# Mixer layer on one core: the dt stage placed in the u projection, conv token work emitted later, Fourier steps started later

## The chip, the cores and the metric

The kernel runs on one core of a Trainium2 chip. The metric is the device time in microseconds (us). A core has a matrix engine (TensorE, PE in the profile), a vector engine (DVE), a scalar engine (ACT), GpSimd (POOL) and SyncE (SP), which in this kernel issues all the DMA transfers. Each engine runs its own queue of instructions in order, and waits at an instruction whose inputs, or whose output buffer, are not ready.

## The reference

One layer with two parallel groups of channels: a Fourier group and a bidirectional chunked scan (SSD). The context, 256 tokens, only feeds the scan's starting states. Cut to what matters:

```python
u, zf, zs, xbc, dt_raw = jnp.split(h @ w_in, PROJ_SPLITS, axis=-1)   # h: normed, modulated tokens
four = fourier_mixer(u, zf, w_fourier, b_fourier)    # Re(fft2(u)) @ w_f + b_f, times silu(zf)
xbc = depthwise_conv_grid(xbc, conv_w, conv_b, rows, cols)           # 3x3 taps, then silu
# ssd_mixer, x/B/C from xbc, two directions:
dt = jax.nn.softplus(dt_raw + dt_bias)
A = -jnp.exp(a_log)
a_cum = jnp.cumsum(dt * A, axis=-1)                  # inside each chunk of 128 tokens
y_diag = einsum(cb, exp(segsum(a)), x * dt)
states = einsum(B, exp(a_cum[..., -1:] - a_cum), x * dt)
y_off = einsum(C, previous_states, exp(a_cum))
y = y_f + flip(y_b) + d_skip * x
out = rmsnorm(y * silu(zs)) * norm_w
x = x + gate * (concat([four, out]) @ w_out)         # then a final rmsnorm
```

There are 2048 latent tokens of width 1024, so 16 latent chunks and 2 context chunks of 128 tokens, and 24 heads in each of two directions (48 columns of dt).

## The kernel before

Data are fp32; a product with fp32 accuracy is made of three products of split operands (high part `h`, low part `l`), so a projection of one 128-wide weight tile onto 512 tokens is 8 x 3 matmuls, L170 to L172. The split of a weight tile (L72) has its high part on ACT and its low part (`wl<-raw,wh`) on POOL. All the work is emitted by one Python program; a scheduler with a model of time then sets the order of the instructions on each engine, and emission order is the priority among what it finds ready. The order on an engine is fixed when the program is built. PE writes to PSUM buffers by kind: five of kind `mm` (called pj or po in the rows), two of kind `tr` (ptr, L152), one of kind `cx`. Evacuation tiles `ev` (L179) and the weight tiles `wh`, `wl` have two buffers each, and these two buffers are used in turn.

The stages, in the order of time:

1. Norm, modulation, the raw dt projection (`dt_block`, which leaves dtT_d in DRAM), and the first two tiles of zf (L183 evacuates them).
2. The u projection, L373 to L393: 16 rounds `n2`. Each has 24 matmuls (L380 to L382), a split of the result, and a DFT group of three matmuls (L388 to L390) through a ptr buffer. At round 2 the context's norm is emitted.
3. The conv stage, L397 to L508: 20 tiles of 128 channels in the order CONV_ORDER, four groups of one C tile, one B tile and three x tiles. Each tile projects four blocks of 512 tokens into a padded image; `finish(half)` (L464) makes the nine taps (one on ACT, L467, eight on DVE, L470) into `acc` and the silu on ACT (L473). Then come the token parts: transposes on PE (L415, `to_tokens`) with an ACT copy to `tk` and a store to xtok_d; for B tiles also a split into `sh` and `sl` (ACT, then POOL) with stores to bhl_d, and the C·B products (L445). For C tiles the split and the stores to chl_d are made from acc. `sh` and `sl` hold eight chunks in one buffer each.
4. The dt stage, L522 to L610: all of dt for nine chunks at a time (NH = 9), two halves one after another, in pools of its own. Per half: dtT is loaded, a matmul a chunk with the matrix `i2` sums the high and low rows (L547; the trace has two records of each, 36 in all), about 15 steps on DVE and ACT make softplus, dt·A (`da`, L569), then the cumulative sums on PE (L572 with `triu` and `tril`, L575 with `ones`), exponentials, and 9 or 7 transposes each of `cum` and `lq` (L602), whose results go as `th` (ACT, L68) and `tl` (DVE, L606), one buffer each, to DRAM (cum_d, q_d), at most four chunks at a time. `sml` (state weights and total decay), `ecb` and `dsc` stay in SBUF for the scan; the whole is also stored to sm_d for the main stage.
5. The scan stage, L664 to L760: 16 context units and then 64 steps of the backward direction. A unit loads x and B, weighs x on POOL (`xw`, L686), splits it (`xh` on ACT, `xl` on DVE), and makes three matmuls of 384 columns (L716 to L718); POOL and DVE update the state (L725, L726). From the first latent chunk on, `scan_off` adds the output products (L698 to L700). The remaining zf and zs projections (`zs_ops`, L618) are emitted between the steps by `interleave` (L649) to fill PE.
6. The Fourier stage, L789 to L950: tables `f_table` (L835), the second DFT step, and the mixing products `f_mm`, interleaved with the last blocks of zs by the same function: `interleave(main, side, lead, speed)` emits the side steps only once `lead` microseconds of its modelled main work are out, and then at the rate `speed`.
7. The main stage: units that join the two directions and the output projection (L1008 to L1143).

Of the kernel before, what the change touches and what calls it, by code (L numbers as in the profile page):

```python
# [18 lines left out]
P = 128  # L19
# [7 lines left out]
H = 24  # L27
# [22 lines left out]
def mixer_layer(ctx: ExitStack, tc: tile.TileContext, A: dict, out: bass.AP, taps=None):  # L50
# [299 lines left out]
    with ExitStack() as pu:  # L350
# [46 lines left out]
    with ExitStack() as pc_:  # L397
# [28 lines left out]
        def hl_tiles():  # L426
            return [cp.tile([P, 8, P], F32R, name=nm, tag=nm, bufs=1) for nm in ("sh", "sl")]
# [27 lines left out]
        def conv_tile(n, ci):  # L455
# [8 lines left out]
            def finish(half):  # L464
# [10 lines left out]
                if kind == "x":  # L475
                    x_tokens(sof, j, c0, 8)
                elif kind == "B":
                    b_tokens(sof, j, c0, 8)
                    cb_products(sof, cso[half], j, c0)
                else:  # L480
                    cso[half] = sof
                    parts = hl_tiles()
                    split(*parts, sof.rearrange("p (c w) -> p c w", w=P), nc.gpsimd)
                    hl_store(chl_d, parts, c0, 8, j)
# [37 lines left out]
    pre1 = preload(LNEXP)  # L522
    with ExitStack() as pd, tc.issue_after(pre1):
        sm = pool("smd", stack=pd)
        tp = pool("tpd", stack=pd)
        triu = const_tile("triu", where=sm)
        tril = const_tile("tril", where=sm)
        ones = const_tile("ones", where=sm)
        alog = const_tile("alog", where=sm)
        dtb = const_tile("dtb", where=sm)  # L530
        i2 = const_tile("i2", where=sm)
        dsk = const_tile("dskip", where=sm)
        nega = sm.tile([P, W2], F32, name="nega")
        nc.scalar.activation(nega, alog, AF.Exp)
        nc.vector.tensor_scalar(out=nega, in0=nega, scalar1=-1.0, scalar2=None, op0=ALU.mult)
        NH = NALL // 2
        for hf_ in range(2):
            sl = slice(NH * hf_, NH * hf_ + NH)

            def small(tag):  # L540
                return tp.tile([P, NH, W2], F32, name="t_" + tag, tag=tag)

            dtT = tp.tile([2 * W2, NH * P], F32, name="dtT", tag="dtT", bufs=1)
            load(dtT, dtT_d[:, NH * P * hf_:NH * P * (hf_ + 1)])
            pt = tr_psum([P, NH, W2])
            for q in range(NH):
                mm(pt[:, q, :], dtT[:, q * P:(q + 1) * P], i2, start=True, stop=True)  # L547
            v, e, u, s1_, same, da, cum = (small(t) for t in ("v", "e", "u", "s1", "same", "da", "cum"))
            smx = tp.tile([P, NH, 2, W2], F32, name="smx", tag="smx", bufs=1)
            wdec, etot = (sml[:, sl, i] for i in range(2))  # L550
            ecum, dtt = (smx[:, :, i] for i in range(2))

            def bc(t):
                return t[:].unsqueeze(1).broadcast_to([P, NH, W2])

            nc.vector.tensor_tensor(out=v, in0=pt, in1=bc(dtb), op=ALU.add)
            nc.vector.scalar_tensor_tensor(out=e, in0=v, scalar=-1.0, in1=v, op0=ALU.mult, op1=ALU.max)
            nc.scalar.activation(e, e, AF.Exp, scale=-1.0)
            nc.vector.tensor_scalar(out=u, in0=e, scalar1=1.0, scalar2=None, op0=ALU.add)
            nc.scalar.activation(s1_, u, AF.Ln)  # L560
            nc.vector.tensor_scalar(out=u, in0=u, scalar1=-1.0, scalar2=None, op0=ALU.add)
            nc.vector.tensor_scalar(out=same, in0=u, scalar1=0.0, scalar2=None, op0=ALU.is_equal)
            nc.vector.tensor_tensor(out=u, in0=u, in1=same, op=ALU.add)
            nc.vector.tensor_tensor(out=s1_, in0=s1_, in1=same, op=ALU.add)
            nc.vector.reciprocal(out=u, in_=u)
            nc.vector.tensor_tensor(out=s1_, in0=s1_, in1=u, op=ALU.mult)
            nc.vector.tensor_tensor(out=s1_, in0=s1_, in1=e, op=ALU.mult)
            nc.vector.scalar_tensor_tensor(out=dtt, in0=v, scalar=0.0, in1=s1_, op0=ALU.max, op1=ALU.add)
            nc.vector.tensor_tensor(out=da, in0=dtt, in1=bc(nega), op=ALU.mult)  # L569
            for d, tri in enumerate((triu, tril)):  # L570
                pt = tr_psum([P, NH, H])
                mm(pt, tri, da[:, :, d * H:(d + 1) * H], start=True, stop=True)  # L572
                nc.vector.tensor_copy(out=cum[:, :, d * H:(d + 1) * H], in_=pt)
            pt = tr_psum([P, NH, W2])
            mm(pt, ones, da, start=True, stop=True)  # L575
            nc.scalar.activation(etot, pt, AF.Exp)
            nc.vector.tensor_tensor(out=wdec, in0=pt, in1=cum, op=ALU.subtract)
            nc.scalar.activation(wdec, wdec, AF.Exp)
            nc.vector.tensor_tensor(out=wdec, in0=wdec, in1=dtt, op=ALU.mult)
            nc.scalar.activation(ecum, cum, AF.Exp)  # L580
            lq = small("lq")
            nc.vector.tensor_scalar(out=lq, in0=dtt, scalar1=1e-37, scalar2=None, op0=ALU.max)
            nc.scalar.activation(lq, lq, AF.Ln)
            nc.vector.tensor_tensor(out=lq, in0=lq, in1=cum, op=ALU.subtract)
            c1 = min(NCH, NH * (hf_ + 1))
            nl, cl = c1 - NH * hf_, slice(NH * hf_, c1)
            nc.gpsimd.tensor_copy(out=ecb[:, cl], in_=ecum[:, :nl, H:])
            dv = dsc[:, cl]
            nc.vector.tensor_tensor(out=dv, in0=dtt[:, :nl, H:].rearrange("p c (g h) -> p c g h", g=G),
                                    in1=cbd[:, cl].unsqueeze(3).broadcast_to([P, nl, G, HG]), op=ALU.mult)  # L590
            dv = dv.rearrange("p c g h -> p c (g h)")
            nc.vector.tensor_tensor(out=dv, in0=dv, in1=dsk[:].unsqueeze(1).broadcast_to([P, nl, H]), op=ALU.add)
            store(sm_d[sl, :, 0:2].rearrange("c p i w -> p c i w"), sml[:, sl])
            store(sm_d[sl, :, 2:4].rearrange("c p i w -> p c i w"), smx)
            for src, dst in ((cum, cum_d), (lq, q_d)):
                c0 = NH * hf_
                while c0 < min(NH * (hf_ + 1), NCH):
                    nq = min(4, min(NH * (hf_ + 1), NCH) - c0)
                    n = nq * P
                    pt = tr_psum([W2, 512])  # L600
                    for q in range(nq):
                        nc.tensor.transpose(pt[:, q * P:(q + 1) * P], src[:, c0 + q - NH * hf_, :], ident)  # L602
                    th = tp.tile([W2, 512], F32R, name="th", tag="th")
                    tl = tp.tile([W2, 512], F32R, name="tl", tag="tl")
                    copy(th[:, :n], pt[:, :n])
                    nc.vector.tensor_tensor(out=tl[:, :n], in0=pt[:, :n], in1=th[:, :n].bitcast(F32), op=ALU.subtract)  # L606
                    cs = slice(c0 * P, c0 * P + n)
                    store(dst[0, :, cs].bitcast(F32), th[:, :n].bitcast(F32))
                    store(dst[1, :, cs].bitcast(F32), tl[:, :n].bitcast(F32))
                    c0 += nq  # L610
# [692 lines left out]
```

## Time and profile before

| | before |
|---|---|
| runs, median (lowest to highest) | 2002.3 us (1998.61 to 2002.57), 3 runs |
| the profiled execution, its own time | 1995.1 us |
| its span | 1993.2 us |
| stage 1 | 0 to 118 us, PE busy 98.69 |
| stage 2, u projection | 118 to 231 us, PE busy 113.00 of 113 |
| stage 3, conv | 231 to 806 us, PE busy 547.89 of 575 |
| stage 4, dt, to the first scan unit's weighing | 806 to 889 us, PE busy 51.19 of 83, mean clock 0.78 |
| stage 5, scan | 889 to 1187 us, PE busy 283.66 of 298, mean clock 0.94 |
| stage 6, Fourier | 1187 to 1340 us, PE busy 141.76 of 153 |
| stage 7, main units | 1340 to 1993.2 us, PE busy 599.58 of 653.2 |

All the rows come from one profiled execution; its times count from the start of its span. An engine is called busy while an instruction runs on it. A row of the timeline gives start, duration, engine, line, operation and tiles, and in brackets how long the engine stood idle before and what released it. The clock is the share of full TensorE speed that the chip granted. Matmuls overlap in the pipeline, so the distance between two starts, not the duration in a row, is the pace.

### The profile page before, as it was taken

How to read it: one execution, taken by the hardware profiler on the slowest of the kernel's cores; microseconds unless marked ns; L12 is line 12 of the kernel's file. 1: busy time of each engine (PE TensorE's matmuls, PEld its weight loads, DVE VectorE, ACT ScalarE, POOL GpSimd, SP SyncE). 2: the span in 40 equal slices, each digit the busy share in tenths (PEclk: the TensorE clock that was granted, in tenths of full speed). 3: DMA queues.
4: the chain of work that ended last, by engine and by line, in shares of the span. 5: the costliest groups of instructions: out<-in, count | busy, mean ns of one | idle time of the engine just before them, and what ended most of it. 6: DMA issues, size and time to landing. Idle time of an engine off the chain costs nothing.

```text
span 1993.2 us, 27660 instructions
## 1 busy us (share of the span) xinstructions
PE 1835.8 (92%) x9136; PEld 1507.1 (76%) x9136; DVE 1382.5 (69%) x1820; ACT 868.2 (44%) x1932; POOL 918.8 (46%) x760
## 2 busy tenths in 40 slices
PE   6999999999999999938999989988899999999997
PEld 2799987877878878726788877866687777778775
DVE  3742399898998998447667651247877787787874
ACT  3531143434443434325666653325544344444433
POOL 1321133131140241108777762247867676877742
PEclk8999999999999999957999999998899999999999
DMA  7332133232232332436777765466544444454441
GB/s 273 131 94 76 34 96 93 70 99 71 76 98 72 88 101 58 139 102 198 219 227 229 222 204 188 143 202 196 177 139 125 132 148 123 134 157 132 135 141 46
DMA packets 267679, 268.47 MB, mean 135 GB/s; under 512 B 27057, under 2 KB 235537, under 8 KB 267026
## 3 DMA queue, kind: packets, MB, share of 16 engines
q1 hardware_dynamic: 267538, 266.72, 44.2%
q8 instruction: 73, 1.20, 0.3%
q14 instruction: 68, 0.56, 0.1%
HBM read 180.10 MB, written 86.54 MB: 134 GB/s over the span
## 4 chain that ended last, share of the span: by engine, by line
PE 37%; DVE 7%; DMA 6%; POOL 3%; ACT 2%; issue 2%; SPq 1%; DVEq 0%; ACTq 0%; POOLq 0%
PE po L1143 5%; PE po L1142 5%; PE po L1141 5%; PE pj L170 4%; PE pj L172 4%; PE pj L171 4%; PE py L1082 2%; PE parg L1008 1%; DMA wo<-in_wout 1%; PE py L1085 1%; DMA xg<-xtok_d 1%; PE ptr L849 1%; SPq L63 1%; DVE gt L1107 1%; PE pn L1098 1%
## 5 line engine op out<-in xcount | busy, mean ns | idle before, releaser
L470 DVE SCALAR_TENSOR_TENSOR acc<-img,c_convw,acc 128x1024 f32<-128x1024 f32 x320 | 485.6, 1524 | 49.2 <-ACT acc L467 39.6
L172 PE MATMUL pj<-hh,wl 128*128 128x512 f32 x1152 | 455.4, 395 | 0.0
L171 PE MATMUL pj<-hl,wh 128*128 128x512 f32 x1152 | 454.4, 394 | 0.0
L170 PE MATMUL pj<-hh,wh 128*128 128x512 f32 x1152 | 453.5, 398 | 0.0
L72 POOL TENSOR_TENSOR wl<-raw,wh 128x1024 fp32r<-128x1024 f32 x48 | 122.9, 2561 | 402.8 <-ACT wh L68 402.8
L172 PEld LDWEIGHTS pj<-hh,wl 128*128 128x128 f32 x1152 | 218.5, 190 | 45.9 <-issue 0.5
L170 PEld LDWEIGHTS pj<-hh,wh 128*128 128x128 f32 x1152 | 219.4, 190 | 42.0 <-issue 1.8
L171 PEld LDWEIGHTS pj<-hl,wh 128*128 128x128 f32 x1152 | 218.6, 190 | 41.1 <-issue 2.1
L1141 PE MATMUL po<-hl,mh 128*128 128x512 f32 x384 | 156.2, 407 | 3.8 <-ACT mh L68 3.1
L1142 PE MATMUL po<-hh,mh 128*128 128x512 f32 x384 | 152.5, 397 | 3.9 <-DVE hh L786 3.9
L1143 PE MATMUL po<-hl,ml 128*128 128x512 f32 x384 | 146.7, 400 | 3.6 <-POOL ml L72 3.6
L703 ACT ACTIVATE xd<-xt,dsc 128x64 f32<-128x64 f32 x384 | 101.3, 336 | 75.9 <-POOL yb L706 69.8
L473 ACT ACTIVATE acc<-acc,c_convb 128x1024 f32<-128x1024 f32 x40 | 46.1, 1152 | 160.4 <-DVE acc L470 160.4
L1012 ACT ACTIVATE w<-parg 128x384 f32<-128x384 f32 x128 | 62.3, 487 | 110.0 <-DVE parg L1010 109.6
L1008 PE MATMUL parg<-rt,lt 128*128 128x384 f32 x256 | 89.6, 374 | 13.2 <-DVE parg L1010 7.0
L1013 DVE TENSOR_TENSOR w<-w,cb 128x768 f32<-128x768 f32 x64 | 85.9, 1342 | 13.1 <-ACT w L1012 12.3
L68 ACT ACTIVATE xh<-xw 128x384 fp32r<-128x384 f32 x136 | 70.2, 517 | 56.7 <-POOL xw L686 25.1
L72 POOL TENSOR_TENSOR ml<-gt,mh 128x384 fp32r<-128x384 f32 x64 | 69.4, 1084 | 54.4 <-ACT mh L68 48.1
L686 POOL TENSOR_TENSOR xw<-xt,sml 128x384 f32<-128x384 f32 x76 | 68.4, 901 | 52.8 <-DVE xl L72 32.5
L1051 POOL TENSOR_TENSOR ts<-ts,yb 128x384 f32<-128x384 f32 x64 | 73.8, 1154 | 40.8 <-issue 18.3
L1010 DVE COPY_PREDICATED parg<-msk,parg 128x384 f32<-128x384 uint8 x128 | 70.8, 553 | 30.3 <-PE parg L1008 30.2
L68 ACT ACTIVATE tk<-ptr 128x512 f32<-128x512 f32 (+1 forms) x96 | 51.3, 556 | 88.7 <-PE ptr L415 50.6
(384 smaller groups left out, 4083.2 us busy)
## 6 DMA issues: line engine op xcount, KB each, us to landing
raw<-in_win SPq DMA_DIRECT2D x48, 512.0 KB
xt<-xtok_d SPq DMA_DIRECT2D x80, 192.0 KB
xtok_d<-tk SPq DMA_DIRECT2D x48, 256.0 KB
zsT_d<-ev SPq DMA_DIRECT2D x48, 256.0 KB
yb_d<-yb SPq DMA_DIRECT2D x64, 192.0 KB
yb<-yb_d SPq DMA_DIRECT2D x64, 192.0 KB
zs<-zsT_d SPq DMA_DIRECT2D x64, 192.0 KB
xg<-xtok_d SPq DMA_DIRECT2D x64, 192.0 KB
```

What stands on the lines that cost most here:

```text
L68: return nc.scalar.activation(dst, src, AF.Copy).ins
L72: (lo_engine or nc.vector).tensor_tensor(out=lo, in0=src, in1=hi.bitcast(F32), op=ALU.subtract)
L170: mm(po, wh[:, k], a, start=(k == 0), stop=False)
L171: mm(po, wh[:, k], b, start=False, stop=False)
L172: mm(po, wl[:, k], a, start=False, stop=(k == KT - 1))
L470: nc.vector.scalar_tensor_tensor(out=acc, in0=im[:, r0 + dy:r0 + dy + 16, dx:dx + GRID_W], scalar=tap(t), in1=acc, op0=ALU.mult, op1=ALU.add)
L703: nc.scalar.activation(xd[:, h], d["x"][:, h], AF.Copy, scale=dsc[:, c, g, h:h + 1])
L1008: mm(po, l[:, dr], r[:, cols], start=True, stop=True)
L1013: nc.vector.tensor_tensor(out=w, in0=w, in1=cb[:].unsqueeze(1).broadcast_to([P, HG, P]), op=ALU.mult)
L1141: mm(po, a, wh[:, i], start=(g == 0 and q == 0), stop=False)
L1142: mm(po, a, wl[:, i], start=False, stop=False)
L1143: mm(po, b, wh[:, i], start=False, stop=(g == 3 and q == 3))
```

## The change

1. **dt stage.** The block L522 to L610 is gone. Its constants are loaded at the start of the u projection (`dt_consts`, into pieces of the weight buffers `wh` and `wl`, which are unused there), and its work is done by `dt_part(i)` in three parts of six chunks, emitted in rounds 4, 7 and 10 of the u projection. `dtT`, `th` and `tl` are taken from the two `ev` tiles, and the outputs from the tile `rawv`. All four results of a part are stored to sm_d, 48 columns (192 bytes) a piece. After conv, `sml`, `ecb` and `dtb2` (dt of the backward direction) are loaded back from sm_d, and `dsc` is computed in two DVE instructions. The step that made the mask `same` is folded into the two additions. The switch of ACT's function table in front of the dt stage is gone.
2. **conv.** `finish` now returns a function `go` with the token part of its half. The list `late` keeps it until behind the next odd block's projection and copy. `sh` and `sl` hold four chunks instead of eight, still one buffer each, and are split and stored four chunks at a time.
3. **Fourier.** `interleave` gets a lead of 10 and a speed of .75 where it had 0 and .7.

```diff
+        NH = NALL // 3
+        def dt_consts():
...
+            flat = [W["p"].tile([P, KT, P], F32R, name=t, tag=t)[:].rearrange("p a b -> p (a b)").bitcast(F32)
+                    for t in ("wh", "wl")]
...
+        def dt_part(i):
+            sl = slice(NH * i, NH * i + NH)
+            out3 = um.tile([P, 2, 512], F32, name="rawv", tag="rawv")[:].rearrange("p a b -> p (a b)")
...
+            pt = tr_psum([P, NH, W2])
+            for q0 in range(0, NH, 4):
+                nq = min(4, NH - q0)
+                dtT = evac_tile()[:2 * W2, :nq * P]
+                load(dtT, dtT_d[:, (NH * i + q0) * P:(NH * i + q0 + nq) * P])
+                for q in range(nq):
+                    mm(pt[:, q0 + q, :], dtT[:, q * P:(q + 1) * P], D0["i2"], start=True, stop=True)
...
+            for d, tri in enumerate(("triu", "tril")):
+                mm(pt[:, :, d * H:(d + 1) * H], D0[tri], da[:, :, d * H:(d + 1) * H], start=True, stop=True)
...
+            mm(pt, D0["ones"], da, start=True, stop=True)
...
+            for q, t in enumerate((wdec, etot, ecum, dtt)):
+                store(sm_d[sl, :, q].rearrange("c p w -> p c w"), t)
+            for src, dst in ((cum, cum_d), (lq, q_d)):
+                c0 = NH * i
+                while c0 < min(NH * (i + 1), NCH):
...
+                    pt = tr_psum([W2, 512])
+                    for q in range(nq):
+                        nc.tensor.transpose(pt[:, q * P:(q + 1) * P], src[:, c0 + q - NH * i], ident)
+                    th, tl = (evac_tile()[:W2].bitcast(F32R) for _ in range(2))
...
+        dt_consts()
         for n2 in range(16):
             if n2 == 2:
                 ctx_block()
+            if n2 in (4, 7, 10):
+                dt_part((n2 - 4) // 3)
...
-            return [cp.tile([P, 8, P], F32R, name=nm, tag=nm, bufs=1) for nm in ("sh", "sl")]
+            return [cp.tile([P, 4, P], F32R, name=nm, tag=nm, bufs=1) for nm in ("sh", "sl")]
...
+                if b % 2 and late:
+                    late.pop(0)()
                 if b == 2:
-                    finish(0)
+                    late.append(finish(0))
                 if b == 3:
-                    finish(1)
+                    late.append(finish(1))
...
-        NH = NALL // 2
-        for hf_ in range(2):
...
-                    th = tp.tile([W2, 512], F32R, name="th", tag="th")
-                    tl = tp.tile([W2, 512], F32R, name="tl", tag="tl")
...
+    load(sml, smr[:, :, 0:2])
+    load(ecb, smr[:, :NCH, 2, H:])
+    load(dtb2, smr[:, :NCH, 3, H:])
...
-    left = interleave(zs_ops([(i, (3,)) for i in range(19, 7, -1)]), side, 0, .7)
+    left = interleave(zs_ops([(i, (3,)) for i in range(19, 7, -1)]), side, 10, .75)
```

In the changed kernel the lines are other ones: the u products are L474 to L476, the DFT group L482 to L484, the dt products L414, L433, L436 and L455 (before: L547, L572, L575, L602), th and tl L457 and L458, conv's transposes L509; the scan's xw L710, its output products L722 to L724, its unit products L740 to L742.

What the built programs hold shows two places. First PE's queue in the u projection of before, where `pj<-wuh,hh` and its neighbours are u products and `h_dft`, `l_dft` the DFT matrix:

```order
L380 MATMUL pj<-wuh,hh 128x512
L381 MATMUL pj<-wul,hh 128x512
L388 MATMUL ptr<-uh,h_dft_1088 128x512
L382 MATMUL pj<-wuh,hl 128x512
L380 MATMUL pj<-wuh,hh 128x512
L381 MATMUL pj<-wul,hh 128x512
L389 MATMUL ptr<-ul,h_dft_1088 128x512
L390 MATMUL ptr<-uh,l_dft_1089 128x512
L382 MATMUL pj<-wuh,hl 128x512
```

The DFT products of a round are spread among the u products of the next one. Now PE's queue around the first dt part of the changed kernel, where `wh` and `wl` are dt's scratch (da in `wh`, the constants in `wl`):

```order
L476 MATMUL pj<-wuh,hl 128x512
L433 MATMUL ptr<-wh,wl 128x6x24 x2
L436 MATMUL ptr<-wh,wl 128x288
L455 MATMUL ptr<-c_ident,wh 48x128 x12
L482 MATMUL ptr<-uh,h_dft_1088 128x512
L483 MATMUL ptr<-ul,h_dft_1088 128x512
L484 MATMUL ptr<-uh,l_dft_1089 128x512
L482 MATMUL ptr<-uh,h_dft_1088 128x512
L483 MATMUL ptr<-ul,h_dft_1088 128x512
L484 MATMUL ptr<-uh,l_dft_1089 128x512
L482 MATMUL ptr<-uh,h_dft_1088 128x512
```

The sums, all twelve transposes of the part and three DFT groups stand together, without a u product among them, and all write to the two ptr buffers. The second part stands in the same way; the third has eight transposes. Ahead of L433 of the three parts stand 40, 54 and 54 u or conv projection products, counted from the part's L414 products.

Second, PE's queue at the head of the scan before (`t_da`, `t_cum`, `t_lq` are dt tiles, `pj<-hh,wh` a zf or zs projection, `xh_6215,bb_6211` the first scan unit):

```order
L172 MATMUL pj<-hh,wl 128x512
L572 MATMUL ptr<-t_da,c_triu 128x216
L572 MATMUL ptr<-t_da,c_tril 128x216
L575 MATMUL ptr<-t_da,c_ones 128x432
L602 MATMUL ptr<-c_ident,t_cum 48x128 x9
L602 MATMUL ptr<-c_ident,t_lq 48x128 x9
L547 MATMUL ptr<-c_i_5980,dtT 128x48 x9
L572 MATMUL ptr<-t_da,c_triu 128x216
L572 MATMUL ptr<-t_da,c_tril 128x216
L575 MATMUL ptr<-t_da,c_ones 128x432
L602 MATMUL ptr<-c_ident,t_cum 48x128 x7
L602 MATMUL ptr<-c_ident,t_lq 48x128 x7
```

Behind these rows the first unit's L716 follows at once, and 14 units stand with no projection between them. The same place of the changed kernel:

```order
L172 MATMUL pj<-hh,wl 128x512
L170 MATMUL pj<-hh,wh 128x512
L171 MATMUL pj<-hl,wh 128x512
L740 MATMUL ptr<-xh_6304,bb_6300 128x384
L172 MATMUL pj<-hh,wl 128x512
L170 MATMUL pj<-hh,wh 128x512
L741 MATMUL ptr<-xl_6305,bb_6300 128x384
L742 MATMUL ptr<-xh_6304,bb_6300 128x384
L740 MATMUL ptr<-xh_6314,bb_6310 128x384
L171 MATMUL pj<-hl,wh 128x512
L741 MATMUL ptr<-xl_6315,bb_6310 128x384
L742 MATMUL ptr<-xh_6314,bb_6310 128x384
```

The first unit now follows straight on a projection and shares the queue with it. On SP's queue the loads of the scan stand behind these rows now:

```order
L63 DMA xtok_d<-tk 128x4x128 x2
L63 DMA zfT_d<-ev 128x512
L63 DMA c_dskip<-in_dskip 128x24
L63 DMA sml<-sm_d 128x18x96
L63 DMA ecb<-sm_d 128x16x24
L63 DMA dtb_6284<-sm_d 128x16x24
L63 DMA c_ones<-in_ones 128x128
L63 DMA xt_6298<-xtok_d 128x384
L63 DMA bb_6300<-bhl_d 128x256
```

Before, ten stores of th, tl, smx and sml stood in front of the load of the first unit's xt there; now it is one zf store and the reload from sm_d.

More of the change, by code (lines that the diff above doesn't have):

```diff
@@ L371, in ctx_block, with cut @@
                 dt_block(ctx_psum()[:2 * W2], hch, hcl, 0, CTX, SEQ)
+        D0 = {}
+        NH = NALL // 3
+        def dt_consts():
+            sz = NH * W2
+            flat = [W["p"].tile([P, KT, P], F32R, name=t, tag=t)[:].rearrange("p a b -> p (a b)").bitcast(F32)
+                    for t in ("wh", "wl")]
+            def cut(f, names, size):
+                for nm in names:
+                    D0[nm] = flat[f][:, :size]
+                    flat[f] = flat[f][:, size:]
+            cut(0, ("v", "e", "u"), sz)
+            cut(0, ("i2", "dtb", "nega"), W2)
+            cut(1, ("s1", "dtt"), sz)
+            cut(1, ("triu", "tril", "ones"), P)
+            cut(1, ("alog",), W2)
+            for nm in ("triu", "tril", "ones", "alog", "dtb"):
+                load(D0[nm], A[nm])
+            D0["i2"] = D0["i2"][:2 * W2]
+            load(D0["i2"], A["i2"])
+            with tc.issue_after(pre):
+                nc.scalar.activation(D0["nega"], D0["alog"], AF.Exp)
+            nc.vector.tensor_scalar(out=D0["nega"], in0=D0["nega"], scalar1=-1.0, scalar2=None, op0=ALU.mult)
@@ L474, in finish, with go @@
                 c0 = 8 * half
[L475 to L484, printed above, removed]
+                def go():
+                    if kind == "x":
+                        x_tokens(sof, j, c0, 8)
+                    elif kind == "B":
+                        b_tokens(sof, j, c0, 8)
+                        cb_products(sof, cso[half], j, c0)
+                    else:
+                        cso[half] = sof
+                        for q in range(0, 8, 4):
+                            parts = hl_tiles()
+                            split(*parts, sof[:, P * q:P * (q + 4)].rearrange("p (c w) -> p c w", w=P), nc.gpsimd)
+                            hl_store(chl_d, parts, c0 + q, 4, j)
+                return go
             for b in range(4):
@@ L505, in conv_tile @@
             (x_tokens if kind == "x" else b_tokens)(acc, j, NCH, NCC)
+        late = []
         for n, ci in enumerate(CONV_ORDER):
             conv_tile(n, ci)
+        for fn in late:
+            fn()
     p1c.close()
@@ L521, in mixer_layer @@
     zf_tile(2)
[L522 to L535, printed above, removed]
-        NH = NALL // 2
-        for hf_ in range(2):
[L538 to L602, printed above, removed]
-                    th = tp.tile([W2, 512], F32R, name="th", tag="th")
-                    tl = tp.tile([W2, 512], F32R, name="tl", tag="tl")
[L605 to L610, printed above, removed]
@@ new lines, in mixer_layer @@
+    dtb2 = pers.tile([P, NCH, H], F32, name="dtb2")
+    dsk = const_tile("dskip", pers)
+    smr = sm_d[:].rearrange("c p i w -> p c i w")
+    load(sml, smr[:, :, 0:2])
+    load(ecb, smr[:, :NCH, 2, H:])
+    load(dtb2, smr[:, :NCH, 3, H:])
+    nc.vector.tensor_tensor(out=dsc, in0=dtb2[:].rearrange("p c (g h) -> p c g h", g=G),
+                            in1=cbd[:].unsqueeze(3).broadcast_to([P, NCH, G, HG]), op=ALU.mult)
+    dv = dsc[:].rearrange("p c g h -> p c (g h)")
+    nc.vector.tensor_tensor(out=dv, in0=dv, in1=dsk[:].unsqueeze(1).broadcast_to([P, NCH, H]), op=ALU.add)
```

46 lines of the change are left out of this document (43 added, 3 removed).

## The prediction

> **What bounds the kernel now.** I read the page first, then the busy time by windows, the waits of TensorE (PE) in the worst stretch, and the timelines there.
>
> ```profile
> span 1993.2 us, 27660 instructions
> ## 1 busy us (share of the span) xinstructions
> PE 1835.8 (92%) x9136; PEld 1507.1 (76%) x9136; DVE 1382.5 (69%) x1820; ACT 868.2 (44%) x1932; POOL 918.8 (46%) x760
> ...
> PEclk8999999999999999957999999998899999999999
> ```
>
> PE is busy for 92% of the span, so time is won only where it waits or runs at a lowered clock. The two low digits of PEclk (5 and 7) are slices 18 and 19 of 49.8 us each, 847 to 947 us. In the windows the columns are the stretch, its length, PE, PEld, DVE, ACT and POOL busy, the clock, the DMA share and GB/s:
>
> ```profile
> 200.00:220.00 20.00, 20.00 (x85) 19.60 (x85) 4.47 (x7) 1.80 (x3) 0.00 (x0) 1.00 0.14 39
> 806.40:917.20 110.80, 69.66 (x271) 50.92 (x270) 50.90 (x82) 34.94 (x64) 27.55 (x28) 0.71 0.47 138
> 860.00:880.00 20.00, 7.14 (x29) 5.09 (x29) 13.03 (x22) 6.27 (x9) 0.33 (x1) 0.58 0.07 21
> ```
>
> The u projection (200:220) is all PE at full clock. The head of the scan, from the last transposes of conv to the first output product (L698, which starts at the second window's end), takes 110.8 us at a mean clock of 0.71. What PE waits for there (us, times, longest):
>
> ```profile
> PE ptr L572 <- DVE t_da L569: 11.2, 1, 11.2
> PE ptr L716 <- ACT xh L68: 10.2, 2, 9.8
> PE ptr L602 <- DVE tl L606: 7.8, 4, 2.7
> PE ptr L602 <- DVE sml L577: 4.5, 2, 2.9
> ```
>
> All but the second are the dt stage's, and the second is the first scan unit, whose loads stand behind that stage's stores on SP. The timeline of PE, with start, duration and the wait ahead in brackets:
>
> ```profile
> 803.81 0.39 PE L170 MATMUL pj<-hh,wh 128*128 128x512 f32 x1
> ...
> 805.17 0.40 PE L170 MATMUL pj<-hh,wh 128*128 128x512 f32 x1
> ...
> 847.13 1.26 PE L602 MATMUL ptr<-c_ident,t_cum 128*48 128x128 f32 x5 [2.88 <-DVE sml L577]
> ...
> 858.47 4.08 PE L547 MATMUL ptr<-c_i,dtT 96*128 96x48 f32 x18 [2.29 <-DVE tl L606]
> 873.75 1.08 PE L572 MATMUL ptr<-t_da,c_triu 128*128 128x216 f32 x2 [11.21 <-DVE t_da L569]
> ```
>
> Six projection products go from 803.81 to 805.17: 0.227 us each at full clock.
>
> **Part 1: dt leaves the scan head.** In this stretch the old order has 146 projection products, then the dt products, then 14 scan units of three products in a row. The new one has 147 products and the 14 units, of which 0 to 6 are spread between products and 7 to 13 stand together. The prices of the units:
>
> ```profile
> 1184.81 0.34 PE L699 MATMUL pj<-sl,cc 128*128 128x384 f32 x1
> 1184.99 0.34 PE L700 MATMUL pj<-sh,cc 128*128 128x384 f32 x1
> ```
>
> ```profile
> 908.42 0.83 POOL L686 TENSOR_TENSOR xw<-xt,sml 128x384 f32<-128x384 f32 x1 [0.49 <-DVE xl L72]
> ```
>
> ```profile
> L72 POOL TENSOR_TENSOR wl<-raw,wh 128x1024 fp32r<-128x1024 f32 x48 | 122.9, 2561 | 402.8 <-ACT wh L68 402.8
> ```
>
> Products: 147 x 0.227 = 33.4. Units: 42 products of 384 columns, 0.18 each at full clock = 7.6. Units 7 to 13 go at the pace of POOL's xw, 0.83 + 0.49 = 1.32 a unit against 0.54 on PE: 7 x 0.78 = 5.5. The lo weights of the next tile (wl, 2.56) now stand in POOL's queue among the xw: 2.6. One drop of the clock: 1.7 (part 2). The first unit now needs sml back from DRAM; with ecb and dtb2 that is 18 x 128 pieces of 384 bytes and 2 x 16 x 128 of 96, 6400 in all. The dt stores of before, in 844 to 852 us, price a piece (packets, MB, share of 16 engines):
>
> ```profile
> q1 hardware_dynamic: 3070, 1.47, 69.1%
> ```
>
> 3070 packets of 479 bytes on average took 0.691 x 8 = 5.5 us, 1.8 ns each, so 6400 take 11.5. The new order puts 83 products, 18.8 us, ahead of unit 0. On SP the reload stands behind the last token stores and a zf store, the unit's own loads stand behind it, and then comes the chain xw, xh, xl. I estimate 3 us of wait, between none and the whole 11.5. Sum: 33.4 + 7.6 + 5.5 + 2.6 + 1.7 + 3 = 53.8 against 110.8: **-57** (-66 without the wait and at PE's own pace, -40 with all 14 units at POOL's pace and the whole wait).
>
> **Part 2: dt inside the u projection.** PE is never idle there, so each wait is new, and the projection stands behind it in PE's queue. The DVE chain up to da (the 11.21 us before 873.75, for nine chunks) is about 7.5 for six; 40 products (9.1 us) or more lie between L414 and L433 and hide it, and DVE has 4.47 us of other work in 20. The tail isn't hidden: L433, L436, twelve transposes and three DFT groups stand in a row, all through the two ptr buffers. The second half of before has the same shape, four pairs of th (ACT) and tl (DVE):
>
> ```profile
> 881.52 0.48 ACT L68 ACTIVATE th<-ptr 48x384 fp32r<-48x384 f32 x1 [1.95 <-DMA cum_d<-th]
> 884.07 0.59 ACT L68 ACTIVATE th<-ptr 48x512 fp32r<-48x512 f32 x1 [2.07 <-DMA cum_d<-th]
> 886.69 0.48 ACT L68 ACTIVATE th<-ptr 48x384 fp32r<-48x384 f32 x1 [2.03 <-DMA q_d<-th]
> ```
>
> ```profile
> 887.51 0.55 DVE L606 TENSOR_TENSOR tl<-ptr,th 48x384 fp32r<-48x384 f32 x1 [2.13 <-DMA q_d<-tl]
> ```
>
> A pair takes 2.6 us, 2.0 of it until the last pair's store has landed: th and tl have one buffer each, and in the new code they take the two ev tiles, so again one pair at a time. From L572 (873.75) to the end of the last tl (888.06) are 14.3 us. The third DFT group needs the buffer that this tl frees; the two groups ahead of it are 6 x 0.227 = 1.4 of old work. Four stores to sm_d now stand on SP among the pairs' own, estimated at one more 1.5. So 14.3 - 1.4 + 1.5 = 14.4 for parts 1 and 2 each. The third has two pairs (only chunks up to 15 go out): 14.3 - 2 x 2.6 - 1.4 = 7.7. The L414 products: 18 took 4.08 at half clock, so 36 take 4.1 at full. And the clock:
>
> ```profile
> 424.00:426.00 2.00, 2.00 (x6) 1.52 (x5) 1.96 (x3) 1.92 (x5) 0.00 (x0) 0.50 0.00 0
> 847.00:848.00 1.00, 0.86 (x5) 0.65 (x5) 0.96 (x3) 0.56 (x1) 0.00 (x0) 0.50 1.14 319
> ```
>
> ```profile
> L171 PE MATMUL pj<-hl,wh x3: 395/628/628, 423.7 to 426.2; 128*128 128x512 f32 x3
> ```
>
> After the 2.88 us wait before 847.13 the clock stands at 0.50. After a conv wait it did too (424:426), and six products (three of them L171) took from 423.7 to 426.2, 1.2 us over their full pace; with the transposes ahead of them I estimate 1.7 a drop, three drops 5.1. Sum: 2 x 14.4 + 7.7 + 4.1 + 5.1 = **+46**. Lower bound: the PE work alone, about 11 (36 + 32 small products at 0.11, three L436 groups), and per part one wait of 2.9 and one drop: +24. Upper: the chain from 858.47 to 888.06, 29.6 us for nine chunks, times 2/3, three times: +59. I take the sum by rows, somewhat above their middle, since the order leaves no projection product between the transposes and the DFT groups. POOL is idle there, and SP's weight loads use 0.14 of the DMA.
>
> The Trainium skill, page "TensorE: Matmul & The Clock Gate", section "HAM oscillation — how this bites in real kernels", gives as the rule that only idle gaps above about 3.4 us throttle the array. By it the pauses here, mostly below 3 us each, would cost no clock and this term would be 41. The window after 847 disagrees (0.50 after a gap of 2.88), so the drops stay in.
>
> **Part 3: conv.** All that PE waits for an acc there, and two of the waits:
>
> ```profile
> PE ptr L415 <- ACT acc L473: 25.8, 12, 4.0
> ```
>
> ```profile
> 325.52 0.87 PE L415 MATMUL ptr<-c_ident,acc 128*128 128x128 f32 x6 [2.51 <-ACT acc L473]
> ...
> 750.59 0.90 PE L415 MATMUL ptr<-c_ident,acc 128*128 128x128 f32 x3 [2.52 <-ACT acc L473]
> ```
>
> The part behind the next block gives ACT and DVE time only where the transposes now stand later on PE, and the scheduler had deferred most of them already: between a half's last input and its transposes stand 57 products before and 57 now for a B tile's first half in the later groups, 45 and 45 for most x tiles. More stand only for x tiles of the first group (44 to 71) and for the second half of the first x tile of each later group (71 to 81). To these belong four waits up to 325.52, which I put at twice that row with the smaller ones, and three like 750.59: 5 + 7.6, about 13 of 25.8. Their clock is worth 1 to 2, and the smaller sh and sl cost as much: **-13** (-30, all of it with its clock, to -5).
>
> **Part 4: Fourier.**
>
> ```profile
> 1195.73 2.05 PE L835 MATMUL pj<-gl,c_c 128*128 128x512 f32 x2 [9.18 <-DMA gl<-in_wf]
> ```
>
> PE waits 9.18 us for the first table load and pays a drop of 1.7. With the lead of 10, 39 to 50 zs products (8.9 to 11.3 us) come before it: **-9** (-12 to -5). The products that this pushes to the tail are the same work.
>
> **Sum.** -57 + 46 - 13 - 9 = -33. The profiled execution took 1995.1 us (span 1993.2), 7.2 below the runs' median of 2002.3; I take the same distance for both kernels: 1962 for a profile like this one, **1969** on the median. A measurement of this kernel can tell about 0.2%, 4 us.
>
> **The rivals.**
>
> *The pauses in u are mostly hidden.* If PE pays the +24 there and conv gains 20, the sum is -57 + 24 - 20 - 9 = -62: 1940. For it: DVE and ACT have little else to do there. Against it: the DFT groups stand right behind the transposes.
>
> *The scan head still waits.* If a piece of 96 bytes costs more than one of 479, or all units go at POOL's pace, only 35 is saved: -35 + 46 - 13 - 9 = -11, so 1991. For it: those pieces and POOL's queue. Against it: the 83 products in front.
>
> *Slower: conv waits for sh and sl.* They had room for eight chunks, now four, still in one buffer, so the next piece starts when the stores of the last have landed. A piece is a split like th (0.59), half a wl on POOL (1.28) and a landing (2.05): 3.9 us, 36 pieces (C 16, B 20), 140 us if PE saw it all.
>
> ```profile
> POOL sl L72 <- ACT sh L68: 106.8, 16, 12.0
> ```
>
> At 24% seen, 33 us, the other gains are gone; at half, 70, the sum is +37: 2039. For it: a B tile's transposes on PE wait for this chain through the ptr buffers. Against it: five pj buffers of 24 x 0.227 = 5.4 us each lie between, and of these 106.8 us on POOL nothing stood in PE's list but the 25.8 for acc.
>
> *The conv edit changes next to nothing,* as most rows of the order say: that is the -5 end of part 3, inside the forecast.
>
> **How the numbers follow.** Forecast 0.63, hidden pauses 0.17, late scan head 0.11, sh and sl 0.06; 0.03 is left over. The forecast's own range, its terms partly cancelling, is 1947 to 1991; with the first two rivals 8 in 10 lie in 1936 to 1996. Faster: 0.60 + 0.17 + 0.08 + 0.01 = 0.86. Same: 0.02 + 0.03 + 0.01 = 0.06. Slower: 0.01 + 0.06 + 0.01 = 0.08.
>
> **What would show it.** Right: from the last conv transposes to the first output product about 54 us; three places in u with 8 to 16 us of PE idle, ended by tl, at a lowered clock; about 12 us of PE waits for acc in conv; none over 2 us for gl. Wrong: u at full clock throughout; a first scan unit more than 5 us late; ACT's sh or POOL's sl ending PE's long waits in conv; or main units that take longer by what was saved.

## The result, and the profile after

The changed kernel takes 1951.44 us (median of 4 runs, 1950.2 to 1953.2), the kernel before 2000.45 (median of its 4 runs by then, 1998.33 to 2002.57): a ratio of 0.9756, 95% interval 0.9739 to 0.9773, so faster by 2.4%. Its profiled execution took 1953.2 us. The page of the changed kernel:

```profile
span 1951.2 us, 27816 instructions
## 1 busy us (share of the span) xinstructions
PE 1826.5 (94%) x9142; PEld 1498.0 (77%) x9142; DVE 1374.8 (70%) x1830; ACT 863.6 (44%) x1940; POOL 919.3 (47%) x766
...
PEclk9999799999999999998999999999999999999998
```

The two low digits of the scan head (5 and 7) are gone; a new 7 stands in the fifth slice, 195 to 244 us, in the u projection. Where the time went I read from the starts of a few rows that both kernels have, which cut a span into stages without gaps (us; all in profiled executions):

| stage, from and to | before | changed | difference |
|---|---|---|---|
| start to first u product | 118.0 | 116.6 | -1.4 |
| u: to last u product | 105.4 | 134.2 | +28.8 |
| conv: to last acc transposes | 582.8 | 585.4 | +2.6 |
| head: to first output product | 111.1 | 53.1 | -58.0 |
| scan: to first table product | 278.4 | 283.6 | +5.2 |
| Fourier: to first main product | 141.6 | 128.4 | -13.2 |
| main units, to the end | 655.9 | 649.9 | -6.0 |
| span | 1993.2 | 1951.2 | -42.0 |

The windows of the changed kernel at one dt part, at the scan head and ahead of the first table product (columns as above):

```profile
188.40:204.00 15.60, 8.44 (x31) 5.24 (x29) 6.42 (x12) 4.69 (x10) 0.00 (x0) 0.73 0.42 97
836.20:889.30 53.10, 45.08 (x193) 35.90 (x191) 22.74 (x35) 16.36 (x33) 26.25 (x26) 0.93 0.81 226
1160.00:1173.00 13.00, 12.27 (x55) 9.89 (x55) 1.11 (x2) 3.80 (x5) 6.75 (x4) 1.00 0.56 169
```

The head was 111 us at a clock of 0.71; it is 53 us at 0.93, with PE busy for 45. What PE waits for there (836 to 890 us, the four longest):

```profile
PE ptr L740 <- DVE hf L750: 2.3, 1, 2.3
PE ptr L740 <- DMA bb<-bhl_d: 2.2, 1, 2.2
PE pj L722 <- ACT sh L68: 2.1, 1, 2.1
PE ptr L740 <- issue: 0.9, 1, 0.9
```

Nothing of dt is left, and sml, back from DRAM, isn't among the releasers. The first unit starts without a wait, 19.0 us behind the last conv transposes at 836.2, so the reload lies under the 83 products in front of it:

```profile
855.16 0.33 PE L740 MATMUL ptr<-xh,bb 128*128 128x384 f32 x1
```

PE's timeline of the first dt part in u:

```profile
188.44 0.65 PE L433 MATMUL ptr<-wh,wl 128*128 128x144 f32 x4
188.92 0.65 PE L436 MATMUL ptr<-wh,wl 128*128 128x288 f32 x2
189.64 0.62 PE L455 MATMUL ptr<-c_ident,wh 128*48 128x128 f32 x4
190.63 0.40 PE L455 MATMUL ptr<-c_ident,wh 128*48 128x128 f32 x2 [0.37 <-DVE rawv L438]
191.66 0.62 PE L455 MATMUL ptr<-c_ident,wh 128*48 128x128 f32 x4 [0.63 <-DVE ev L458]
195.05 0.40 PE L455 MATMUL ptr<-c_ident,wh 128*48 128x128 f32 x2 [2.77 <-DVE ev L458]
197.86 0.79 PE L482 MATMUL ptr<-uh,h_dft 128*128 128x512 f32 x1 [2.41 <-DVE ev L458]
...
200.42 0.80 PE L482 MATMUL ptr<-uh,h_dft 128*128 128x512 f32 x1 [0.91 <-DVE ev L458]
...
201.87 0.63 PE L482 MATMUL ptr<-uh,h_dft 128*128 128x512 f32 x1
...
203.15 0.63 PE L474 MATMUL pj<-wuh,hh 128*128 128x512 f32 x1
```

From L433 to the next u product are 14.7 us, of which the nine DFT products would take 2.0 at full clock: 12.7 lost, and 1.3 more until the clock is back at 205.71. The waits of 2.77 and 2.41 end with a tl in an ev tile (L458), as the order had it, and the second DFT group (200.42) waits for the last tl. The row of before has its first th at 878.23 on ACT, behind a load of ACT's function table (the end of its last tl, 888.06, is in the prediction):

```profile
876.06 1.28 ACT L580 ACT_TABLE_LOAD   x1 [1.25 <-DVE t_cum L573]
878.23 0.58 ACT L68 ACTIVATE th<-ptr 48x512 fp32r<-48x512 f32 x1
```

Here the first th starts at 190.31 and the last tl at 199.95, and ACT loads no table from 186 to 206 us:

```profile
190.31 0.58 ACT L68 ACTIVATE ev<-ptr 48x512 fp32r<-48x512 f32 x1
199.95 0.42 DVE L458 TENSOR_TENSOR ev<-ptr,ev 48x256 fp32r<-48x256 f32 x1 [2.14 <-DMA q_d<-ev]
```

In Fourier, the first table product waits 0.73 instead of 9.18:

```profile
1172.88 1.10 PE L859 MATMUL pj<-gl,c_c 128*128 128x512 f32 x2 [0.73 <-DMA gl<-in_wf]
```

And all that PE waits for in conv, 285 to 838 us:

```profile
PE ptr L509 <- ACT acc L567: 18.2, 11, 4.0
PE ptr L509 <- ACT accc L604: 4.1, 3, 1.4
PE ptr L539 <- ACT tk L68: 0.5, 1, 0.5
```

18.2 instead of 25.8 for acc, but 4.1 are new for accc, the context's part of a tile.

### The profile page after: what moved, and what is told of

The parts are those of the page before. It is cut to its first block, busy times and chain, and to the rows that moved or that the text cites. A ratio compares the mean times of both kernels' runs of the same rounds, so it can differ in the third digit from the quotient of the medians.

```text
span 1951.2 us, 27816 instructions
## 1 busy us (share of the span) xinstructions
PE 1826.5 (94%) x9142; PEld 1498.0 (77%) x9142; DVE 1374.8 (70%) x1830; ACT 863.6 (44%) x1940; POOL 919.3 (47%) x766
## 4 chain that ended last, share of the span: by engine, by line
PE 33%; DVE 24%; POOL 8%; DMA 7%; issue 6%; ACT 4%; SPq 1%; POOLq 0%; ACTq 0%; DVEq 0%
DVE acc L564 17%; PE po L1167 5%; PE po L1165 5%; PE po L1166 5%; PE pj L171 3%; PE pj L172 3%; PE pj L170 3%; PE py L1106 2%; DMA wo<-in_wout 2%; DMA xt<-xtok_d 2%; POOL yb L730 1%; PE parg L1032 1%; POOL xw L710 1%; SPq L63 1%; POOL wl L72 1%
## 5 line engine op out<-in xcount | busy, mean ns | idle before, releaser
L564 DVE SCALAR_TENSOR_TENSOR acc<-img,c_convw,acc 128x1024 f32<-128x1024 f32 x320 | 478.8, 1511 | 32.9 <-ACT acc L561 24.3
L710 POOL TENSOR_TENSOR xw<-xt,sml 128x384 f32<-128x384 f32 x76 | 67.0, 883 | 53.8 <-DVE xl L72 38.9
L1037 DVE TENSOR_TENSOR w<-w,cb 128x768 f32<-128x768 f32 x64 | 83.3, 1301 | 12.2 <-ACT w L1036 11.4
L72 POOL TENSOR_TENSOR sl<-hf,sh 128x384 fp32r<-128x384 f32 x64 | 77.4, 1210 | 22.8 <-ACT sh L68 19.9
```

The costliest lines, as they stand in the source:

```text
L72: (lo_engine or nc.vector).tensor_tensor(out=lo, in0=src, in1=hi.bitcast(F32), op=ALU.subtract)
L564: nc.vector.scalar_tensor_tensor(out=acc, in0=im[:, r0 + dy:r0 + dy + 16, dx:dx + GRID_W], scalar=tap(t), in1=acc, op0=ALU.mult, op1=ALU.add)
L710: nc.gpsimd.tensor_tensor(out=xw, in0=xt, in1=wd, op=ALU.mult)
L1037: nc.vector.tensor_tensor(out=w, in0=w, in1=cb[:].unsqueeze(1).broadcast_to([P, HG, P]), op=ALU.mult)
```

## The experiments

Each run stands beside runs of the kernel before on the same chip; its ratio goes with a 95% interval.

### One edit at a time

`dt_only` is the kernel before with the dt stage moved, `conv_only` with the conv edit, `fourier_only` with the lead and speed, `no_conv` the changed kernel without the conv edit. The edits are those of the diff; for `fourier_only`, for example:

```diff
-    left = interleave(zs_ops([(i, (3,)) for i in range(19, 7, -1)]), side, 0, .7)
+    left = interleave(zs_ops([(i, (3,)) for i in range(19, 7, -1)]), side, 10, .75)
```

> The kernel before with only the dt stage moved (conv and Fourier as before). Theory by the two profiles: the scan head gains 58 and the u projection with its third part loses 36, so -22, a ratio near 0.989. Rival, the sizes of the prediction: -57 + 46 = -11, a ratio near 0.9945. If dt alone already gives all of the change, the ratio is 0.976.

> The kernel before with only the conv edit (late token parts, sh and sl of four chunks). Theory: PE's waits in conv fall by some 4 to 5 us, ratio 0.998. Rival, the prediction's size: -13, ratio 0.9935. Rival, the smaller sh and sl cost more than the late parts gain: ratio above 1.000.

> The kernel before with only the lead of 10 and the speed of .75. Theory: the 9.2 us wait for the first table and its clock drop go, -8 to -11, ratio 0.995. Rival, the wait turns up elsewhere in the Fourier stage or the first main units: ratio 1.000.

> The changed kernel without the conv edit (dt moved, Fourier later, conv as before). Theory: as the changed kernel but 4 to 5 us slower, so a ratio of 0.978 to 0.979 to the kernel before. Rival, the prediction's size of conv: 0.982. Rival, the conv edit and the moved dt stage hang together (what stands at the end of conv sets what fills the scan head): 0.985 or more.

The kernel before had a median of 1998.63 here.

| | median us | ratio (interval) | u | conv | head | scan | Fourier | main |
|---|---|---|---|---|---|---|---|---|
| before (profile) | | | 105.4 | 582.8 | 111.1 | 278.4 | 141.6 | 655.9 |
| dt_only | 1970.09 | 0.9851 (0.9834 to 0.9868) | 132.4 | 590.1 | 52.6 | 279.8 | 139.9 | 653.6 |
| conv_only | 1985.92 | 0.9931 (0.9919 to 0.9944) | 105.4 | 570.6 | 112.4 | 278.1 | 140.3 | 657.1 |
| fourier_only | 1987.72 | 0.9943 (0.9928 to 0.9958) | 105.3 | 582.7 | 111.7 | 280.6 | 128.5 | 656.1 |
| no_conv | 1961.64 | 0.9814 (0.9800 to 0.9828) | 134.5 | 590.1 | 53.4 | 281.3 | 128.6 | 653.5 |

Alone, dt is worth 28.5 us, conv 12.7, Fourier 10.9; the sum of 52.1 is close to the 49.0 of all three. Both sizes that I had for dt (22 and 11) were too small; the one for Fourier (8 to 11) held. My theory for conv, 4 to 5 us read from the two full profiles, fell: alone it gives 12.7, as the prediction had it. PE's list of waits in `conv_only`, 225 to 836 us:

```profile
PE ptr L415 <- ACT acc L473: 13.0, 7, 2.3
PE ptr L415 <- ACT accc L510: 6.2, 4, 2.1
```

The 25.8 for acc have become 13.0, but 6.2 for accc are new, and the clock is lowered less. Summing the busy time times the missing share of the clock over windows of 2 us, the conv stage of before loses 6.3 us to a lowered clock, that of `conv_only` 1.5. Fewer waits (27.1 to 20.0 idle) and a better clock are the 12.2 us of that stage. On top of the moved dt stage the same edit gives 590.1 - 585.4 = 4.7 in the stage and 10.2 on the medians (1961.64 to 1951.44, in different batches of runs); the stage agrees with my theory, the medians come nearer to the prediction's size. Most of the difference of the two is in the main units (653.5 and 649.9), which the edit doesn't touch; see below.

So the gains don't add stage by stage. In u and conv together dt alone costs 34.3 (`dt_only`) and the conv edit alone saves 12.2, which would leave 22.1; the changed kernel loses 31.4. On the medians little of these 9 us is seen, in part because the main units came out shorter (by 6.0, where the three single edits have -2.3, +1.2 and +0.2).

### Does the third dt part eat the conv edit's gain?

The third part's tail falls into the first conv tile. `parts_369` emits the parts a round earlier:

```diff
-            if n2 in (4, 7, 10):
-                dt_part((n2 - 4) // 3)
+            if n2 in (3, 6, 9):
+                dt_part((n2 - 3) // 3)
```

> The changed kernel with the three dt parts emitted in rounds 3, 6 and 9 instead of 4, 7 and 10, so that the third part's tail stands ahead of the first conv tile. Theory, the third part delays the first conv tiles and thereby eats most of the conv edit's gain: the stage from the last u product to the last conv transposes falls from 585 to 575 or less and the sum by 4 to 7 us, ratio 0.972 to 0.974. Rival, the tail costs the same wherever it stands: u grows by what conv loses, ratio 0.9756 as the changed kernel.

Measured: 1954.57 us, ratio 0.9772 (0.9744 to 0.9800); u 136.5, conv 582.6, together 719.1 against 719.6 in the changed kernel. The theory fell: the tail costs about the same wherever it stands. What the moved dt adds to u and conv together is 34.3 without the conv edit (`dt_only` against before, 722.5 to 688.2) and 43.6 with it (the changed kernel against `conv_only`, 719.6 to 676.0). Why the two edits cost 9 us together that neither costs alone stays open.

### What makes the pauses in u

`four_pieces` gives parts 1 and 2 four tiles for th and tl, cut from the second pair of weight buffers. PE's order at the first part stays as it is; at the second, two of the nine DFT products move behind the L414 products of the third part:

```diff
+            pcs = []
+            if i < 2:
+                for t in ("wh", "wl"):
+                    f = W["p"].tile([P, KT, P], F32R, name=t, tag=t)[:].rearrange("p a b -> p (a b)")
+                    pcs += [f[:W2, :512], f[:W2, 512:]]
...
-                    th, tl = (evac_tile()[:W2].bitcast(F32R) for _ in range(2))
+                    th, tl = (pcs[2 * (c0 - NH * i > 0) + q] if i < 2 else evac_tile()[:W2].bitcast(F32R) for q in range(2))
```

> The changed kernel with four th/tl tiles in parts 1 and 2 (cut from the second pair of weight buffers) instead of two; order of PE's queue the same. Theory, the pauses in the u projection are the landing of one store pair after another: of the 12.7 us that PE waits for tl in parts 1 and 2 most goes, 8 to 12 us faster than the changed kernel, ratio to before 0.970 to 0.972. Rival, the pace is set by the two ptr buffers and the chain transposes, th, tl: the waits shrink by 3 us or less, ratio 0.974 to 0.976.

Measured: 1947.97 us, ratio 0.9733 (0.9705 to 0.9762), between the two that were expected; u 128.3 instead of 134.2. Its timeline has one long wait a part instead of two; the first part's rows with a wait:

```profile
191.18 0.40 PE L460 MATMUL ptr<-c_ident,wh 128*48 128x128 f32 x2 [0.37 <-DVE rawv L438]
192.21 1.10 PE L460 MATMUL ptr<-c_ident,wh 128*48 128x128 f32 x6 [0.63 <-DVE wh L463]
196.18 0.79 PE L487 MATMUL ptr<-uh,h_dft 128*128 128x512 f32 x1 [2.87 <-DVE wh L463]
```

With four tiles the third pair still takes those of the first and waits for its store. `six_pieces` gives the third pair the two ev tiles:

```diff
+                    if i < 2 and pair != 2:
+                        th, tl = pcs[pair % 3 * 2:pair % 3 * 2 + 2]
+                    else:
+                        th, tl = (evac_tile()[:W2].bitcast(F32R) for _ in range(2))
+                    pair += 1
```

> As the run with four th/tl tiles, but the third pair of parts 1 and 2 takes the two ev tiles, so no pair waits for the store of the pair before it. Theory, what was left of the pauses (2.9 us twice, in front of the first DFT group) was the landing of the first pair's store: it goes too, PE's idle time in the u projection falls from 14 to 3 to 5 us, ratio 0.970 to 0.972. Rival, the chain through two ptr buffers takes the place of the stores: idle time stays above 7 us, ratio as with four tiles.

Measured: 1947.34 us (1936.49 to 1948.75), ratio 0.9714 (0.9686 to 0.9742); u 124.0, PE idle there 5.8 us instead of 14.0. The windows over the whole u stage, of the changed kernel and then of this one:

```profile
116.60:250.80 134.20, 120.23 (x517) 111.09 (x517) 52.41 (x95) 28.43 (x59) 10.91 (x8) 0.92 0.29 76
```

```profile
118.20:242.20 124.00, 118.22 (x516) 109.25 (x516) 52.11 (x95) 28.28 (x59) 10.87 (x8) 0.96 0.31 82
```

So waiting for the stores made 8.2 of the 14.0 us of idle time, and with the clock 10.2 of the 28.8 that u had grown by. A second trace of the changed kernel (`changed_again`, below) has 132.0 for u, so the gain is 8 to 10. The row of sums, transposes and DFT products of each part stayed the same, so the stores are shown to be the cause. Of the 18.6 that are left, 5.8 are waits for ACT and DVE between the steps, 4.4 the lowered clock, and about 8 dt's own work on PE. The medians show less: 3.3 us against the 1950.66 of the changed kernel beside it, with intervals that overlap, since conv and main took longer in this trace (586.3 and 652.8, against 584.7 and 647.9).

### sh and sl: four chunks or eight

`late_hl8` keeps the late token parts but gives sh and sl eight chunks, split and stored as before. It ran twice, the second time beside `changed_again`, the changed kernel itself:

```diff
-            return [cp.tile([P, 4, P], F32R, name=nm, tag=nm, bufs=1) for nm in ("sh", "sl")]
+            return [cp.tile([P, 8, P], F32R, name=nm, tag=nm, bufs=1) for nm in ("sh", "sl")]
...
-                        for q in range(0, 8, 4):
-                            parts = hl_tiles()
-                            split(*parts, sof[:, P * q:P * (q + 4)].rearrange("p (c w) -> p c w", w=P), nc.gpsimd)
-                            hl_store(chl_d, parts, c0 + q, 4, j)
+                        parts = hl_tiles()
+                        split(*parts, sof.rearrange("p (c w) -> p c w", w=P), nc.gpsimd)
+                        hl_store(chl_d, parts, c0, 8, j)
```

> The changed kernel with the late token parts, but sh and sl for eight chunks in one buffer as before. Theory by the waits that are new on ACT and POOL (sh and sl waiting for their own stores, 60 us, none of them on PE): no difference in time, ratio 0.975 to 0.977. Rival from the prediction, the halving exposes a chain of split, store and landing: this is faster by 5 us or more, ratio 0.973 or less. Rival, the halving is what lets the late parts pay: this is slower by 5 us or more, ratio 0.978 or above.

> The changed kernel itself once more, beside the next three on the same chip. All theories: 1950 to 1955 us, ratio 0.975 to 0.977.

> The changed kernel with sh and sl for eight chunks, once more. Theory, no difference that can be told from the changed kernel beside it (within 4 us): the first run's 5 us were main units at a better clock. Rival, the halving costs: 5 us or more faster again, with less PE idle or clock loss in conv.

| | median us | ratio (interval) | conv | main |
|---|---|---|---|---|
| late_hl8 | 1946.31 | 0.9725 (0.9696 to 0.9754) | 582.4 | 645.4 |
| changed_again | 1950.66 | 0.9748 (0.9727 to 0.9769) | 584.7 | 647.9 |
| late_hl8_again | 1944.78 | 0.9720 (0.9698 to 0.9743) | 582.3 | 644.0 |

Twice faster by 5 to 6 us on the medians (the first time against the changed kernel in another batch), with intervals that overlap; the expected "no difference" fell twice. Of this the conv stage has 2.4 to 3.0, both times; the rest is in the main units. PE's waits in conv for `late_hl8_again`:

```profile
PE ptr L509 <- ACT acc L567: 15.5, 10, 4.7
PE ptr L509 <- ACT accc L603: 5.5, 3, 1.8
PE ptr L539 <- ACT tk L68: 0.3, 1, 0.3
```

21.3 in all against 22.8. So the halving costs about 2 to 3 us in conv. The chain that the slower rival feared is in the trace of the changed kernel, but on POOL and ACT (231 to 836 us):

```profile
POOL sl L72 <- DMA chl_d<-sl: 20.4, 8, 2.9
POOL sl L72 <- DMA bhl_d<-sl: 19.5, 8, 3.5
...
ACT sh L68 <- DMA chl_d<-sh: 11.7, 6, 2.2
...
ACT sh L68 <- DMA bhl_d<-sh: 8.5, 3, 3.8
```

60 us of waiting for its own stores, against 7.0 in `late_hl8_again`, and hardly any of it reaches PE.

### The reload, twice

`reload_twice` issues the loads of ecb, dtb2 and sml a second time, 12800 small pieces in all:

```diff
     load(sml, smr[:, :, 0:2])
+    load(ecb, smr[:, :NCH, 2, H:])
+    load(dtb2, smr[:, :NCH, 3, H:])
+    load(sml, smr[:, :, 0:2])
     load(ecb, smr[:, :NCH, 2, H:])
```

> The changed kernel with the three reloads from sm_d issued twice (sml, ecb, dtb2, ecb, dtb2, sml), 12800 small pieces instead of 6400. Theory, the reload is hidden behind the 83 products ahead of the first scan unit and a small piece costs 0.9 ns: 6 us more of DMA, the first unit late by 2 to 6 us, ratio 0.977 to 0.979. Rival, there is more cover than that: ratio 0.9756. Rival, pieces cost 1.8 ns as in the prediction: the first unit is late by 10 us or more, ratio 0.981.

Measured: 1957.22 us, ratio 0.9779 (0.9751 to 0.9806); the head takes 57.1 instead of 53.1. Its list of waits there starts with

```profile
PE ptr L743 <- DMA bb<-bhl_d: 6.8, 5, 4.2
```

where the changed kernel had 2.2. But the run doesn't hold the order: the scheduler knew of the loads, issued them later on SP (from 850.87 on), and put 125 products ahead of the first unit instead of 83. So the first unit waits for nothing here either; the 4.2 is the sixth unit's load of B. Of the 4.0 us of the head, 3.7 are a lower clock (6.0 us lost to it, against 2.3). So the size that I expected came, but not by a late first unit, and how near one reload is to showing, this run can't tell. The price of a piece is in the changed kernel's DMA from 844 to 848 us, when ecb and dtb2 come in:

```profile
DMA packets 4650, 0.61 MB, mean 152 GB/s; under 512 B 4582, under 2 KB 4650, under 8 KB 4650
## 3 DMA queue, kind: packets, MB, share of 16 engines
q1 hardware_dynamic: 4650, 0.61, 102.9%
```

4650 pieces, mostly of 96 bytes, in 4 us of all 16 engines: 0.9 ns each, half of the prediction's 1.8, which came from pieces of 479 bytes on average.

### A version that beats both

`six_hl8` has the tiles of `six_pieces` and the sh and sl of `late_hl8`.

> Both edits together, the version that should beat both kernels. Theory: the six-tile gain alone, 1940 to 1945 us, ratio 0.970 to 0.972. Rival, both edits count: 1935 to 1939 us, ratio below 0.9695.

Measured: 1939.53 us (1936.19 to 1941.72), ratio 0.9691 (0.9670 to 0.9712), beside 0.9748 (0.9727 to 0.9769) for the changed kernel in the same batch: about 11 us faster than the change. Its u stage takes 124.0 and its conv 582.4, so the two gains stand side by side.

## Why the prediction was right, and where its sizes were off

The sign, the places and the mechanisms were right, and 1951.44 lies in the range (1936 to 1996); the change is larger than forecast, -49 for -33. Point by point:

- **Scan head, -57:** measured -58.0 in the changed kernel, -58.5 in `dt_only`. The sum of 53.8 us met 53.1, partly by luck: the first unit's wait (3) did not come, the wl (2.6) does not stand among PE's waits, and waits for the state update, bb and sh (7.9 with the smaller ones) stood in their place. The reload was hidden as forecast. The end of -40 of its range is a slip: its own terms give -43.
- **dt in u, +46:** the step that was mis-sized. By `dt_only` it is 27.0 in u and 7.3 in conv, 34.3. Parts 1 and 2 lost 12.7 and 12.3 where the prediction had 14.4. The chain from the sums to the last tl took 11.9 us in part 1 (188.44 to 200.37) instead of 14.3 + 1.5: its front, up to the first th, took 1.9 instead of 4.5 (a table load of 1.28 stood in it on ACT, among other things), and the pairs 10.1 where they had taken 9.8, so the 1.5 added for the stores to sm_d hardly came. Against that, one reading was wrong: the second DFT group, not the third, needed the buffer of the last tl, so one group lay under the chain instead of two (0.7), and the six products behind it ran at half clock (1.4). The third part lost 4.4 where the prediction had 7.7, and no clock drop: from 256 to 264 us the changed kernel ran at 1.00. The sign of 8 to 16 us of idle at each of three places was not met: it was 14.0 at two places together and 1.3 at the third. The mechanism, pairs of th and tl that wait for their stores, is shown by the runs with more tiles.
- **Conv, -13:** `conv_only` gives 12.7, and the waits for acc fell from 25.8 to 13.0 as worked out. The sum is partly luck: 6.2 of new waits for accc were not foreseen, and the clock gave 4.8 where the prediction had 1 to 2. In the changed kernel the stage shows less of the gain, 4.7, and 18.2 of waits for acc instead of the 12 that were to be the sign.
- **Fourier, -9:** `fourier_only` gives 10.9; the stage with the one ahead of it loses 10.9 too (scan +2.2, Fourier -13.1), as products moved from one to the other.
- **The profile and the median:** the prediction put both kernels 7.2 us above their profiled time. The profiled execution of before was simply the lowest of its times by then, that of the changed kernel the highest of its four. That step cost 9 us: against the profile the forecast was 1962 for 1953.2.
- **The rivals:** the slower one (sh and sl) cost 2 to 3 us in conv instead of 70; that PE's other buffers cover the rest is argued, not tested. The late scan head was excluded by the trace. Hidden pauses in u were wrong for this kernel, and became half true with six tiles.

Against the -42.0 of the two spans, the forecast of -33 thus has errors of both signs: dt cost some 11 us less, the conv edit gave 8 us less beside it, and the main units, for which the sum has no term, were 6.0 shorter.

What stays open: the main units took 644.0 to 653.9 us in the versions of the changed kernel, none of which edits them. Summed as above, the lowered clock cost them 6.7 us in `late_hl8_again` and 19.1 in `parts_369`. Whether the program ahead sets this or chance does, these single traces don't tell. Two things speak for the program: the two kernels traced twice came within 2.0 and 1.4 us of themselves there, and all eleven traces with the moved dt stage have shorter main units (up to 653.9) than the three without it (655.9 to 657.1). No run shows by what. So 5 us on a median is not read as an edit's effect here without its own stage showing it.

## What to carry to other kernels

A serial stage of small steps goes under a stage that is bound by one engine only if its steps don't stand in that engine's own queue in front of the next big work: look at the built order for unbroken rows, and price each row by its buffers (here one pair of tiles, 2.6 us a pair until the store has landed; with three pairs the two rows cost 8 to 10 us less together). Cut the span at the same rows in every run: edits that shift work between stages then show their own gain, while the medians move by several microseconds for other reasons.

## What the runs showed of the hardware

The clock does not need one long gap to fall. In `six_hl8` no wait of the first dt part is longer than 0.92 us:

```profile
190.00:192.00 2.00, 1.02 (x6) 0.46 (x6) 1.54 (x5) 1.81 (x5) 0.00 (x0) 1.00 0.25 50
192.00:194.00 2.00, 1.02 (x6) 0.46 (x6) 1.37 (x4) 0.59 (x1) 0.00 (x0) 1.00 1.00 188
194.00:196.00 2.00, 1.18 (x4) 0.69 (x5) 0.72 (x3) 0.95 (x2) 0.00 (x0) 1.00 0.84 173
196.00:198.00 2.00, 2.00 (x6) 1.39 (x6) 2.00 (x4) 0.60 (x1) 0.00 (x0) 0.61 0.42 110
198.00:200.00 2.00, 2.00 (x6) 1.61 (x5) 0.25 (x1) 0.60 (x1) 0.00 (x0) 0.54 0.84 248
200.00:202.00 2.00, 2.00 (x10) 2.00 (x10) 1.08 (x2) 0.00 (x0) 0.00 (x0) 1.00 0.59 170
```

PE was busy for 3.2 of the 6 us up to 196, in short pieces, and then ran at 0.61 and 0.54 through 4 us of unbroken work. But such a stretch need not do it. In `six_pieces` the same row, with the same waits to within 0.04 us, was busy for 3.25 of the same 6 us, and the clock stayed at 1.00:

```profile
191.19:197.19 6.00, 3.25 (x16) 1.64 (x17) 3.66 (x9) 3.37 (x8) 0.00 (x0) 1.00 0.69 136
197.19:199.19 2.00, 1.99 (x9) 1.44 (x9) 2.00 (x4) 0.87 (x2) 0.00 (x0) 1.00 0.46 114
```

So the same row can cost a drop in one trace and none in the next; what decides it, no run here shows. The Trainium skill, page "TensorE: Matmul & The Clock Gate", section "HAM oscillation — how this bites in real kernels", speaks of idle gaps above about 3.4 us; here a stretch without such a gap, with a busy share of about a half, was enough in one of these two traces.
